# One more projection by seven half-size products: q of the second attention pattern

## The chip, the core and the metric

The kernel runs on one core of a Trainium2 chip. The core has a matrix engine (PE, whose weight loads are shown apart as PEld), three engines for elementwise work (DVE, ACT, POOL) and a queue engine (SP) that mainly issues DMAs; POOL issues DMAs as well. The engines run their instructions in order and wait for one another on semaphores. The metric is device time in microseconds. The kernel before took 2716.3 us, the median of three runs (2712.53, 2716.3 and 2717.81).

## The reference, cut to what matters

The program is a two-layer trunk on a sequence of 1024 rows of width 1024, all in float32. Layer 0 mixes tokens by a gated MLP, layer 1 by dilated attention; a squared-ReLU MLP follows each. The change lies in layer 1, in the making of q, k and v:

```
B_HEADS = 16                       # 64 wide each, so 8 pairs of heads
B_PATTERNS = ((128, 1), (512, 4), (2048, 16))     # window, dilation

def mixer_b(h, w_qkv, w_out, slopes):
    qkv = (h @ w_qkv).reshape(B, S, N_PAT, 3, B_HEADS, B_HEAD_DIM)
    for g, (window, dilation) in enumerate(B_PATTERNS):
        o, lse = dilated_branch(qkv[:, :, g, 0], qkv[:, :, g, 1], qkv[:, :, g, 2],
                                window, dilation, slopes)
```

There are three patterns g = 0, 1, 2, and for each a q, a k and a v: nine products of a 1024x1024 activation and a 1024x1024 piece of `w_qkv`. Pattern 1 has dilation 4: position s of the sequence stands in row i of residue r, with s = 4 i + r, and attention works on the residues apart. So its q, k and v are used in the order (r, i), here called the pattern's order.

## The kernel before, in words

Float32 products are made of three passes: each operand is split into a rounded part hi and a rest lo (`split`, line 100: ACT casts hi, then DVE subtracts to get lo), and hi*hi + hi*lo + lo*hi is summed in PSUM. A pass is a matmul of 128x128 by 128x512.

**The stage of v** (`values`, line 1157). v of all three patterns, and q and k of pattern 0, are made by a scheme of seven products of half-size blocks in place of eight (a Strassen scheme). `V_STEPS` (line 1145) lists (g, X, p): pattern g; X = 0, 1, 2 for q, k, v; p the product, in the order 1, 2, 5, 6, 7, 4, 3. One step is 4 blocks m of 12 matmuls, 48 in all, each block in its own PSUM bank. While step n runs, `right.prepare` makes the hi and lo of the next step's weights (two halves, at m = 0 and m = 2; tiles vrhi and vrlo), and `right.load` issues the loads of the step after. After products 1, 5 and 6 `evict` (line 1241) copies the bank to an SBUF tile (vpart); after 2, 7, 4 and 3 it adds that tile to the bank (not after 4, which is complete in its bank), splits the finished 128x512 block into hi and lo in a tile of the pool `parted` (line 1165, tag `vs`), and POOL stores the tile to DRAM. The pool `parted` has two buffers: the third finished block can be split only when the store of the first has landed. Finished blocks come in a burst of twelve, at the end of every group of seven products: four each after 7, 4 and 3.

**Attention** (`attention`, line 1300). It walks over 24 groups, for each pair of heads pattern 2, then 1, then 0 (`order`). A group has 8 slots of two halves. In a slot stand scores (PE), softmax (DVE and ACT), transposes (PE), their split (ACT, DVE) and the product with v (PE); `merge` joins the three patterns of a pair some slots later on DVE, by weights that go to DRAM and come back spread over partitions (`w_dram`, then the tiles bc). Between them `project` (line 1349) is a stream that makes q and k of patterns 1 and 2 pair by pair: one unit is q or k of one pattern and pair, 16 pieces of 3 matmuls (tiles psq and psk), with its weights loaded, split, and its result split in place into the tiles qhi, qlo, khi, klo in the pattern's order. There are 32 units, 512 pieces. 56 pieces (`lead`) run ahead of the first slot, and then the rest is dealt out evenly: in each half slot a credit of 512 - 56 = 456 is added and each piece costs 351, so 1.30 pieces stand in a half slot, until half slot 351. q and k of pattern 0 are loaded from DRAM, four blocks per pair (`load_block`).

The order on each engine is set by the program text and a scheduler that takes instructions by priority; the instructions marked `keep_in_program_order` stay where they are.

POOL's DMAs have a scratch that the kernel sets to 1024 bytes (`SCRATCH`, line 32, used in line 1843). In the attention pools qk[1] and qk[2], q and k of patterns 1 and 2 have one buffer for each tile.

Of the kernel before, what the change touches and what calls it, by code (L numbers as in the profile page):

```python
# [10 lines left out]
F32 = mybir.dt.float32  # L11
F32R = mybir.dt.float32r
# [23 lines left out]
def trunk(ctx: ExitStack, tc: tile.TileContext, x, c, ada_w, ada_b, ln_g, ln_b, a_w_in, a_b_in,  # L36
# [3 lines left out]
    nc = tc.nc  # L40
# [11 lines left out]
    dram = pool(ctx, "dram", 1, space=DRAM)  # L52
# [47 lines left out]
    def split(hi, lo, src, hi_engine=A, lo_engine=V):  # L100

        first = A.copy(hi, src) if hi_engine is A else hi_engine.tensor_copy(hi, src)  # L102
        return first, lo_engine.tensor_tensor(lo, src, hi, op=ALU.subtract)  # L103
# [994 lines left out]
    v_dram = [dram.tile([S, N_PAIRS, 4 * HEAD], F32, name=f"v_{g}") for g in range(3)]  # L1098

    qk_dram = dram.tile([N_PAIRS, 2, P, 2, S], F32, name="qk_0")  # L1100

    class RightForms:
        BLOCK = {1: (0, 0), 2: (1, 0), 5: (0, 1), 6: (1, 1), 7: (0, 1), 4: (1, 0)}
# [38 lines left out]
            split(hi[:], lo[:], r)  # L1142
            self.ready[g, X, p, kp] = hi, lo

    V_STEPS = [(g, X, p) for g, X in ((2, 2), (1, 2), (0, 2), (0, 0), (0, 1)) for p in (1, 2, 5, 6, 7, 4, 3)]

    def values_ahead(right):
        for kp in range(2):
            right.load(*V_STEPS[0], kp)
        yield  # L1150
        right.prepare(*V_STEPS[0], 0)
        right.load(*V_STEPS[1], 0)
        yield
        right.prepare(*V_STEPS[0], 1)
        right.load(*V_STEPS[1], 1)

    def values(before, right, ahead):
        run(ahead)
        form = before.form
        name = {1: "L11", 2: "L12", 5: "S1", 6: "S2", 7: "S3", 4: "L22", 3: "S4"}  # L1160
        with ExitStack() as ph:
# [3 lines left out]
            parted = pool(ph, "parted_v", 2)  # L1165
# [75 lines left out]
            def evict(g, X, p, m):  # L1241
                acc = sums["pb" if p in (2, 5, 3) else "pa", m][:]
                if p in (1, 5, 6):
                    t = parts[p, m] = x_tile(f"vpart_{g}_{X}_{p}_{m}")
                    A.copy(t[:], acc)
                    return
                if p != 4:
                    t = parts.pop(({2: 1, 7: 5, 3: 6}[p], m))
                    V.tensor_tensor(t[:], acc, t[:], op=ALU.add)  # L1249
                    acc = t[:]  # L1250
                half, dh = {2: (1, 0), 3: (1, 1), 4: (0, 0), 7: (0, 1)}[p]
                if X < 2:
                    t = parted.tile([P, 2, HALF], F32R, name=f"qs_{X}_{p}_{m}", tag="vs")
                    split(t[:, 0], t[:, 1], acc)
                    nc.gpsimd.dma_start(qk_dram[4 * dh + m, X, :, :, half * HALF : (half + 1) * HALF], t[:].bitcast(F32))
                    return
                v = parted.tile([P, 4, 4, HEAD], F32R, name=f"vs_{g}_{p}_{m}", tag="vs")
                split(v[:, :, 0:4:3, :], v[:, :, 1:3, :], acc.rearrange("p (h e c) -> p h e c", e=2, c=HEAD))
                i = 4 * half + m
                nc.gpsimd.dma_start(v_dram[g][i * P : (i + 1) * P, 4 * dh : 4 * dh + 4, :],  # L1260
                                  v[:].rearrange("p h f c -> p h (f c)").bitcast(F32))
# [36 lines left out]
    def attention(form):  # L1298
# [5 lines left out]
        with ExitStack() as ph:  # L1304
# [3 lines left out]
            qk = {g: pool(ph, f"attn_qk{g}", 1, side="right") for g in (1, 2)}  # L1308
# [33 lines left out]
            order = [(hp, g) for hp in range(N_PAIRS) for g in (2, 1, 0)]  # L1342
# [5 lines left out]

            def project():

                todo = [(n, X) for n in range(len(order)) if order[n][1] for X in range(2)]

                raw, units = {}, {}

# [17 lines left out]
                for i, (n, X), half in [(i, key, half) for i, key in enumerate(todo) for half in (1, 0)]:  # L1372
                    hp, g = order[n]
# [7 lines left out]
                    p = bank("mm", f"ps{nm}_{hp}_{g}_{half}")  # L1381
                    for k in range(KD):
# [3 lines left out]
                        if k == KD - 1:  # L1386
                            hi, lo = (perm(got[n][f"{nm}{m}"][:], g, half) for m in ("hi", "lo"))
# [21 lines left out]
            def attend(n, oT_of):  # L1409
                hp, g = order[n]  # L1410
                base = 8 * n
                my = got[n]
# [19 lines left out]
                last_one = n == len(order) - 1  # L1432
                groups = {0: ((0, 1), (2, 3), (4, 5), (6, 7)), 1: ((0, 1, 2), (3, 5), (4, 7, 6)), 2: ((0, 1, 2, 3), (4, 5, 6, 7))}[g]
                starts = {0: (0, 2, 3, 5) if last_one else (0, 2, 4, 6), 1: (0, 2, 5), 2: (0, 4)}[g]

                def load_block(m):
                    my[m] = []
# [355 lines left out]
            out_begin = begin()  # L1793

            stream = project()
            lead, credit = 7 * KD, 0
            for n in range(lead):
                next(stream)
                if 16 <= n < 20:
                    affine_load(n - 16)  # L1800
            due = 0
            for n, slot in enumerate(slots):
                for half, pos in enumerate(slot):
                    for _, f in sorted(pos, key=lambda x_: x_[0]):
                        f()
                    credit += 512 - lead
                    while credit >= 351:
                        credit -= 351
                        next(stream, None)
                    if n >= last_group - 8:  # L1810
                        due += 6
                        while due >= 8:
                            due -= 8
                            next(out_begin, None)
# [41 lines left out]
```

## Time and profile before

| | |
|---|---|
| three runs | 2712.53, 2716.3, 2717.81 us; median 2716.3 |
| profiled execution | 2717.79 us, its span 2716.1 us, mean granted clock of PE 0.996 |
| PE busy | 2655.5 us, 98% of the span |
| DVE, ACT, POOL busy | 1993.0, 1378.4, 114.9 us |
| stage of v | about 992 to 1379 us of the span |
| attention with its lead | from about 1379 us on |

In the profile L1283 stands for the matmuls of the stage of v (psv), L1384 for those of `project`, L102 and L103 for the two halves of every split, L1249 for the addition in `evict`, L1255 and L1260 for POOL's stores of q, k (tile qs) and v (tile vs). Busy time of PE counts pipelined matmuls from their start to a modelled end, so a PE that is 98% busy is one that seldom waits, and what a matmul costs is read from the distance between two starts, not from its duration.

### The profile page before, as it was taken

The page shows a single profiled execution, that of the slowest core. Times are in us where ns is not written, and L with a number is a line of the kernel's source. Part 1 is how long each engine was busy: PE and PEld are TensorE (multiplying, and loading weights), DVE is VectorE, ACT ScalarE, POOL GpSimd, SP SyncE. Part 2 cuts the span into 40 slices and gives each one's busy share as a digit, 9 for nine tenths or more (in the row PEclk, how much of TensorE's full clock was granted, in tenths as well). Part 3 has the DMA queues.
Part 4 walks back from the last instruction along what each step waited for, and adds up shares of the span by engine and source line. Part 5 has one row for each costly group of instructions (what it writes and reads, how often), then busy time and mean ns, then how long its engine had stood idle before and what let it go on. Part 6 is the DMA issues. An engine that isn't in the chain of part 4 may idle for free.

```text
span 2716.1 us, 37099 instructions
## 1 busy us (share of the span) xinstructions
PE 2655.5 (98%) x13242; PEld 2193.5 (81%) x13242; DVE 1993.0 (73%) x3610; ACT 1378.4 (51%) x2601; POOL 114.9 (4%) x193
## 2 busy tenths in 40 slices
PE   6999999999999999999999999999999999999998
PEld 5788887888788878888888888888887888878887
DVE  6787697777889778655647767777658966577877
ACT  3354375555444454433436666666645655544332
POOL 1000000000000001111111000000010000000000
PEclk9999999999999999999999999999999999999999
DMA  7534336667967745655475545554782654495562
GB/s 264 159 118 135 116 137 217 223 223 243 344 229 247 245 148 180 215 179 198 165 225 172 138 133 140 138 146 133 235 219 98 213 190 155 147 317 183 172 208 86
DMA packets 340781, 504.77 MB, mean 186 GB/s; under 512 B 51900, under 2 KB 177252, under 8 KB 340596
## 3 DMA queue, kind: packets, MB, share of 16 engines
q1 hardware_dynamic: 324212, 443.68, 51.5%
q0 software_dynamic: 16384, 58.73, 6.0%
q8 instruction: 104, 1.70, 0.3%
q14 instruction: 81, 0.66, 0.1%
HBM read 365.40 MB, written 136.92 MB: 185 GB/s over the span
## 4 chain that ended last, share of the span: by engine, by line
PE 76%; DVE 12%; DMA 6%; ACT 3%; issue 2%; SPq 0%; DVEq 0%; ACTq 0%
PE psd L957 22%; PE psv L1283 13%; PE psk L1384 6%; PE psq L1384 6%; PE psua L798 6%; DMA adaw<-in_ada_w_dram 3%; PE psd_wout L389 3%; PE pv L1553 3%; PE psuc L798 3%; PE psu L368 3%; PE sc L1473 3%; PE psv L470 2%; DVE adaacc L128 2%; DVE left L103 1%; PE pT L1526 1%
## 5 line engine op out<-in xcount | busy, mean ns | idle before, releaser
L798 PE MATMUL psua<-right,left 128*128 128x512 f32 x1536 | 364.8, 391 | 0.1
L957 PE MATMUL psd<-rhi,lhi 128*128 128x512 f32 x896 | 349.7, 390 | 3.0 <-ACT part L829 3.0
L957 PE MATMUL psd<-rlo,lhi 128*128 128x512 f32 x896 | 349.6, 390 | 0.2
L957 PE MATMUL psd<-rhi,llo 128*128 128x512 f32 x896 | 349.3, 390 | 0.0
L798 PEld LDWEIGHTS psua<-right,left 128*128 128x128 f32 x1536 | 288.3, 188 | 61.6 <-DVE right L103 1.2
L1495 ACT ACTIVATE p<-p,stat 128x128 f32<-128x128 f32 (+1 forms) x384 | 168.8, 441 | 96.8 <-DVE stat L1493 95.8
L957 PEld LDWEIGHTS psd<-rhi,lhi 128*128 128x128 f32 x896 | 168.6, 188 | 39.2 <-ACT part L829 3.9
L957 PEld LDWEIGHTS psd<-rlo,lhi 128*128 128x128 f32 x896 | 168.5, 188 | 35.9 <-DVE rlo L103 1.1
L957 PEld LDWEIGHTS psd<-rhi,llo 128*128 128x128 f32 x896 | 168.6, 188 | 34.9
L798 PE MATMUL psuc<-right,left 128*128 128x512 f32 x768 | 187.2, 390 | 0.0
L128 DVE SCALAR_TENSOR_TENSOR adaacc<-adaw,silu_c,adaacc 128x512 f32<-128x512 f32 x168 | 128.6, 775 | 59.6 <-DMA adaw<-in_ada_w_dram 59.0
L798 PEld LDWEIGHTS psuc<-right,left 128*128 128x128 f32 x768 | 143.6, 188 | 29.9 <-DVE right L103 0.2
L103 DVE TENSOR_TENSOR pTlo<-pT,pThi 128x512 fp32r<-128x512 f32 (+1 forms) x160 | 99.3, 621 | 75.9 <-ACT pThi L102 75.0
L103 DVE TENSOR_TENSOR left<-ws,left 128x512 fp32r<-128x512 f32 x128 | 87.9, 688 | 73.2 <-ACT left L102 71.3
L103 DVE TENSOR_TENSOR llo<-lraw,lhi 128x1024 fp32r<-128x1024 f32 x112 | 136.4, 1218 | 1.5 <-ACT lhi L102 1.5
L102 ACT CAST left<-ws 128x512 fp32r<-128x512 f32 x128 | 79.1, 620 | 104.5 <-DVE ws L719 92.0
L1384 PE MATMUL psk<-form_L,wqk_hi 128*128 128x512 f32 x384 | 126.9, 411 | 0.0
L1384 PE MATMUL psq<-form_L,wqk_hi 128*128 128x512 f32 x384 | 126.4, 410 | 0.0
L102 ACT CAST lhi<-lraw 128x1024 fp32r<-128x1024 f32 x112 | 117.3, 1047 | 9.3 <-PE psd L957 3.3
L1283 PE MATMUL psv<-vrhi,form_S 128*128 128x512 f32 x384 | 120.0, 391 | 1.3 <-DVE vpart L1249 0.8
L1493 DVE CUSTOM_DVE_ANT_0 p<-sc,bias 128x128 f32<-128x128 f32 (+1 forms) x384 | 113.7, 346 | 5.2 <-PE sc L1473 4.9
L102 ACT CAST pThi<-pT 128x512 fp32r<-128x512 f32 (+1 forms) x160 | 84.6, 530 | 60.4 <-PE pT L1526 43.3
(332 smaller groups left out, 6072.3 us busy)
## 6 DMA issues: line engine op xcount, KB each, us to landing
lraw<-forms SPq DMA_DIRECT2D x112, 512.0 KB
adaw<-in_ada_w_dram SPq DMA_DIRECT2D x192, 256.0 KB
up<-in_mlp_w_up_dram SPq DMA_DIRECT2D x64, 512.0 KB
forms<-s SPq DMA_DIRECT2D x128, 256.0 KB
rraw<-in_mlp_w_down_dram SPq DMA_DIRECT2D x64, 512.0 KB
forms<-part SPq DMA_DIRECT2D x96, 256.0 KB
v<-vs POOLq DMA_DIRECT2D x48, 512.0 KB, 3.7
vraw<-in_b_w_qkv_dram SPq DMA_DIRECT2D x42, 512.0 KB
```

Of the source, the lines that this page charges most:

```text
L102: first = A.copy(hi, src) if hi_engine is A else hi_engine.tensor_copy(hi, src)
L103: return first, lo_engine.tensor_tensor(lo, src, hi, op=ALU.subtract)
L128: ins = V.scalar_tensor_tensor(acc[:], raw[:], silu_c[:, k : k + 1], acc[:], ALU.mult, ALU.add)
L368: T.matmul(dst, s[a], m[b], start=(n == 0), stop=(n == last))
L389: T.matmul(p[:], stat[a][:, k, o : o + P], u[b][:, w], start=n == 0, stop=n == count - 1)
L798: T.matmul(acc, w[:, a, k, :], right[p][:, b, k, :], start=p in (1, 2, 5) and k + a + b == 0, stop=k == 3 and a == 1, skip_group_check=True)
L957: ins = T.matmul(sums[kind, m][:], l[a][:, k, m * P : (m + 1) * P], r[b][:, k, :], start=p in (1, 5, 2, 3) and kp + k + a + b == 0, stop=k ...
L1283: T.matmul(acc, rows[:, m * P : (m + 1) * P], cols_, start=p in (1, 2, 5) and kp + k + a + b == 0, stop=kp == 1 and k == 1 and a == 1, ski ...
L1384: T.matmul(p[:], wu[a][:, k * P : (k + 1) * P], h_op(k, half, b), start=k + c_ == 0, stop=k == KD - 1 and c_ == 2)
L1473: T.matmul(banks[e][:, sl], q_[a][rows, tq], k_[b][rows, keys], start=c_ == 0, stop=c_ == 2)
L1493: V.tensor_tensor_reduce(out=pr, in0=banks[e][:, sl], in1=st["bias"][:, width - w :], scale=-0.125, scalar=3e38, op0=ALU.add, op1=ALU.min, ...
L1495: A.activation(pr, pr, AF.Exp, bias=nm, scale=-1.0, accum_out=l)
```

## The change

q of pattern 1 leaves `project` and becomes a group of seven steps in `V_STEPS`, behind v of pattern 0 and ahead of q of pattern 0. A finished block is split with a strided reading of its source, so that hi and lo come out in the pattern's order, and is stored to a new DRAM tensor `q_1`, of [pair, 128, hi or lo, 1024]. The store's rows are four pieces of 128 numbers for each partition; it is issued as two DMAs, one for hi and one for lo. In attention `load_q` loads hi and lo of a pair, eight slots ahead of its group, into the same tiles qhi and qlo. `project` has 24 units (384 pieces) left; the lead is 40 pieces, and the credit deals out 328 pieces over the first 326 half slots and the last 16 over the next 25.

```
-    V_STEPS = [(g, X, p) for g, X in ((2, 2), (1, 2), (0, 2), (0, 0), (0, 1)) for p in (1, 2, 5, 6, 7, 4, 3)]
+    V_STEPS = [(g, X, p) for g, X in ((2, 2), (1, 2), (0, 2), (1, 0), (0, 0), (0, 1)) for p in (1, 2, 5, 6, 7, 4, 3)]
...
                 if X < 2:
-                    t = parted.tile([P, 2, HALF], F32R, name=f"qs_{X}_{p}_{m}", tag="vs")
+                    t = parted.tile([P, 2, HALF], F32R, name=f"qs_{g}_{X}_{p}_{m}", tag="vs")
+                    if g:
+                        hi, lo = (t[:, n].rearrange("p (r i) -> p r i", r=4) for n in range(2))
+                        split(hi, lo, acc.rearrange("p (i r) -> p r i", r=4))
+                        dst = q1_dram[4 * dh + m].rearrange("p a (r i) -> p a r i", r=4)
+                        for n in range(2):
+                            nc.gpsimd.dma_start(dst[:, n, :, half * P : (half + 1) * P], (hi, lo)[n].bitcast(F32))
+                        return
...
-                todo = [(n, X) for n in range(len(order)) if order[n][1] for X in range(2)]
+                todo = [(n, X) for n in range(len(order)) for X in {0: (), 1: (1,), 2: (0, 1)}[order[n][1]]]
...
+                @at(max(0, base - 8), 0)
+                def load_q():
+                    if g != 1:
+                        return
+                    for i, m in enumerate(("qhi", "qlo")):
+                        my[m] = qk[1].tile([P, S], F32R, name=f"{m}_{hp}_1", tag=m)
+                        nc.sync.dma_start(my[m][:].bitcast(F32), q1_dram[hp, :, i, :])
...
-            lead, credit = 7 * KD, 0
+            lead, credit = 5 * KD, 0
...
-                    credit += 512 - lead
-                    while credit >= 351:
-                        credit -= 351
+                    credit += (368 - lead) * 25 if 2 * n + half_of < 326 else 16 * 326
+                    while credit >= 326 * 25:
+                        credit -= 326 * 25
                         next(stream, None)
```

Three places show how the instructions stand. On POOL, at the end of v of pattern 0, before:

```order
L1260 DMA v_0_108<-vs_0_3_1_10256 128x1024
L1260 DMA v_0_108<-vs_0_3_2_10277 128x1024
L1260 DMA v_0_108<-vs_0_3_3_10296 128x1024
L1255 DMA qk_0_111<-qs_0_2_0_10391 256x1x512
L1255 DMA qk_0_111<-qs_0_2_1_10410 256x1x512
```

The same place now, where "128x4x128 x2" are the two DMAs of one block, hi and lo:

```order
L1268 DMA v_0_108<-vs_0_3_2_10278 128x1024
L1268 DMA v_0_108<-vs_0_3_3_10297 128x1024
L1260 DMA q_1_112<-qs_1_0_2_0_10392 128x4x128 x2
L1260 DMA q_1_112<-qs_1_0_2_1_10412 128x4x128 x2
L1260 DMA q_1_112<-qs_1_0_2_2_10436 128x4x128 x2
L1260 DMA q_1_112<-qs_1_0_2_3_10456 128x4x128 x2
L1260 DMA q_1_112<-qs_1_0_7_0_10623 128x4x128 x2
```

Sixteen blocks of q, each with two DMAs of 512 pieces of 512 bytes, have come in ahead of the stores of pattern 0, whose blocks are one DMA of 256 pieces.

On ACT, in the new group: the burst of finished blocks (qs) after products 7, 4 and 3, and between them the casts of the weights of later steps (vrhi_1_0_3: product 3 of the new group; vrhi_0_0_1 and vrhi_0_0_2: products 1 and 2 of q of pattern 0, the next group).

```order
L102 CAST qs_1_0_7_0_10623<-vpart_1_0_5_0_10479 128x512
L102 CAST qs_1_0_7_1_10641<-vpart_1_0_5_1_10496 128x512
L102 CAST qs_1_0_7_2_10664<-vpart_1_0_5_2_10516 128x512
L102 CAST vrhi_1_0_3_0_10687<-v_r22_0_8564 128x1024
L102 CAST vrhi_1_0_3_1_10726<-v_r22_1_8565 128x1024
L102 CAST qs_1_0_7_3_10682<-vpart_1_0_5_3_10533 128x512
L102 CAST qs_1_0_4_0_10703<-psv1_1_0_0_10305 128x512
L102 CAST qs_1_0_4_1_10721<-psv1_1_0_1_10322 128x512
L102 CAST qs_1_0_4_2_10742<-psv1_1_0_2_10341 128x512
L102 CAST vrhi_0_0_1_0_10765<-v_t_0_8562 128x1024
L102 CAST vrhi_0_0_1_1_10807<-v_t_1_8563 128x1024
L102 CAST qs_1_0_4_3_10760<-psv1_1_0_3_10358 128x512
```

The pattern goes on with the first three blocks of product 3 (qs_1_0_3_0 to qs_1_0_3_2), then vrhi_0_0_2_0 and vrhi_0_0_2_1, then the last block. So the weights of product 2 of the next group stand on ACT behind the eleventh block of the burst. For v of pattern 0 the order before is the same, with vs in place of qs.

On PE, in attention, in the fourth pair of heads (psk: pieces of `project`; pT: transposes; pv: product with v), before:

```order
L1384 MATMUL psk_4_2_1_14836<-form_L12_8185,wqk_17_hi_14625 128x512 x2
L1384 MATMUL psk_4_2_1_14836<-form_L12_8185,wqk_17_lo_14626 128x512
L1553 MATMUL pv_6_1_0_14947<-pThi_6_1_0_14887,v_3_1_14666 128x256
L1553 MATMUL pv_6_1_0_14947<-pTlo_6_1_0_14888,v_3_1_14666 128x256
L1553 MATMUL pv_6_1_0_14947<-pThi_6_1_0_14887,v_3_1_14666 128x128
L1553 MATMUL pv_6_1_0_14947<-pTlo_6_1_0_14888,v_3_1_14666 128x128
L1384 MATMUL psk_4_2_0_14953<-form_S1_8627,wqk_17_hi_14625 128x512 x2
L1384 MATMUL psk_4_2_0_14953<-form_S1_8627,wqk_17_lo_14626 128x512
L1384 MATMUL psk_4_2_0_14953<-form_S1_8627,wqk_17_hi_14625 128x512 x2
L1384 MATMUL psk_4_2_0_14953<-form_S1_8627,wqk_17_lo_14626 128x512
L1526 MATMUL pT_6_1_2_14960<-ident_73,p_6_1_4_14891 128x128
L1529 MATMUL pT_6_1_2_14960<-ident_73,p_6_1_5_14803 128x128
```

And now:

```order
L1392 MATMUL psk_4_2_1_15153<-form_L12_8186,wqk_13_hi_14919 128x512 x2
L1392 MATMUL psk_4_2_1_15153<-form_L12_8186,wqk_13_lo_14920 128x512
L1569 MATMUL pv_6_1_0_15256<-pThi_6_1_0_15201,v_3_1_14986 128x256
L1569 MATMUL pv_6_1_0_15256<-pTlo_6_1_0_15202,v_3_1_14986 128x256
L1569 MATMUL pv_6_1_0_15256<-pThi_6_1_0_15201,v_3_1_14986 128x128
L1569 MATMUL pv_6_1_0_15256<-pTlo_6_1_0_15202,v_3_1_14986 128x128
L1392 MATMUL psk_4_2_1_15153<-form_L12_8186,wqk_13_hi_14919 128x512 x2
L1392 MATMUL psk_4_2_1_15153<-form_L12_8186,wqk_13_lo_14920 128x512
L1542 MATMUL pT_6_1_2_15265<-ident_73,p_6_1_4_15205 128x128
L1545 MATMUL pT_6_1_2_15265<-ident_73,p_6_1_5_15120 128x128
```

One piece of `project` stands in each half slot where there were one or two; the rest of the row is unchanged.

More of the change, by code (lines that the diff above doesn't have):

```diff
@@ L1100, in trunk @@
     qk_dram = dram.tile([N_PAIRS, 2, P, 2, S], F32, name="qk_0")
+    q1_dram = dram.tile([N_PAIRS, P, 2, S], F32, name="q_1")
     class RightForms:
@@ L1802, in attention @@
             for n, slot in enumerate(slots):
-                for half, pos in enumerate(slot):
+                for half_of, pos in enumerate(slot):
                     for _, f in sorted(pos, key=lambda x_: x_[0]):
                         f()
-                    credit += 512 - lead
-                    while credit >= 351:
-                        credit -= 351
+                    credit += (368 - lead) * 25 if 2 * n + half_of < 326 else 16 * 326
+                    while credit >= 326 * 25:
+                        credit -= 326 * 25
                         next(stream, None)
```

## The prediction

> **What bounds the kernel now.** I read first the table of busy time by stretch, then the chain that ended last, then POOL's timeline and the landing times of its stores.
>
> The table has for each stretch its length and then the busy time of PE, PEld, DVE, ACT and POOL, the granted clock and the DMA share: two stretches of the stage of v, four pairs of attention, and one twelfth of a pair.
>
> ```profile
> 985.00:1250.00 265.00, 263.67 (x1176) 217.05 (x1175) 185.36 (x244) 122.69 (x175) 26.98 (x50) 1.00 0.57 197
> 1250.00:1385.00 135.00, 135.00 (x597) 111.79 (x596) 71.35 (x87) 55.58 (x78) 21.51 (x32) 1.00 0.56 194
> 1500.00:1900.00 400.00, 399.54 (x2707) 336.58 (x2706) 287.40 (x897) 257.16 (x770) 11.79 (x32) 1.00 0.52 140
> 1598.20:1604.40 6.20, 6.20 (x47) 5.18 (x46) 6.04 (x14) 3.47 (x12) 0.00 (x0) 1.00 0.34 92
> ```
>
> In both stages PE is busy to the last per cent at full clock: whatever takes PE work away shortens the kernel, unless another engine makes PE wait. In attention DVE is at 72% and ACT at 64%, but once in a pair DVE is full (6.04 of 6.20 us). The chain gives PE's true price, in consecutive matmuls of one kind:
>
> ```profile
> 1044.59 334.92 PE psv L1283 x1476
> 1379.51 10.88 PE psq L1384 x48
> ...
> 1561.05 1.49 PE sc L1473 x24
> ...
> 1572.45 1.44 PE psk L1384 x6
> ...
> 1613.80 1.40 PE psq L1384 x6
> ...
> 1859.27 1.49 PE sc L1473 x24
> ```
>
> A matmul costs 334.92 / 1476 = 0.227 us in the stage of v and 10.88 / 48 = 0.227 in the lead; in bursts of six between small matmuls 1.40 to 1.44, so 0.233 to 0.240. The first scores of the second and sixth pair stand 298.2 us apart, so a pair takes 74.6 us.
>
> **PE's sum.** Removed: eight units of 48 matmuls, 384. At 0.227 they cost 87.1 us, at 0.240 92.2. Added: seven steps of 48, 336 x 0.227 = 76.3 us; a step takes 10.9. The difference is 11 to 16 us; the bursts don't vanish but get shorter, which keeps part of their switching, so I take **-13 us**.
>
> **The stores of the new blocks.** This is what I expect to decide. The rows of POOL's DMAs before (count, busy, mean ns; KB and median us to landing; the third line, of the stores of q and k, min/median/max), of the ACT casts that wait for them, and of the work of one finished block:
>
> ```profile
> L1260 POOL DMA_DIRECT2D v<-vs x48 | 25.6, 533 | 277.1 <-DVE vs L103 277.1
> L1255 POOL DMA_DIRECT2D qk<-qs x32 | 21.8, 682 | 131.5 <-DVE qs L103 130.6 <-DVE far L1319 0.9
> DMA to landing us min/median/max: 3.0/3.8/8.9
> v<-vs POOLq DMA_DIRECT2D x48, 512.0 KB, 3.7
> wo_parts<-wo_hi POOLq DMA_DIRECT2D x16, 256.0 KB, 5.0
> ACT vs L102 <- DMA v<-vs: 44.0, 21, 5.7
> L1249 DVE TENSOR_TENSOR vpart<-psv,vpart 128x512 f32<-128x512 f32 x60 | 41.1, 685 | 6.3 <-PE psv L1283 6.3
> L102 ACT CAST vs<-vpart 128x512 fp32r<-128x512 f32 x36 | 22.4, 621 | 56.2 <-DVE vpart L1249 27.9 <-DMA v<-vs 18.8 <-DVE vraw L1136 3.7
> L103 DVE TENSOR_TENSOR vs<-vpart,vs 128x512 fp32r<-128x512 f32 x36 | 24.8, 689 | 10.8 <-ACT vs L102 10.8
> L102 ACT CAST vrhi<-v_t 128x1024 fp32r<-128x1024 f32 x28 | 29.2, 1053 | 8.1 <-PE psv L1283 8.1
> L103 DVE TENSOR_TENSOR vrlo<-v_t,vrhi 128x1024 fp32r<-128x1024 f32 x28 | 34.2, 1221 | 18.0 <-ACT vrhi L102 18.0
> ```
>
> And a burst of twelve on POOL's timeline (start, duration), v of pattern 0, with the two closest stores of the next group:
>
> ```profile
> 1199.82 0.53 POOL L1260 DMA_DIRECT2D v<-vs  x1 [22.17 <-DVE vs L103]
> ...
> 1233.01 0.54 POOL L1260 DMA_DIRECT2D v<-vs  x1 [2.93 <-DVE vs L103]
> ...
> 1293.12 0.68 POOL L1255 DMA_DIRECT2D qk<-qs  x1 [5.62 <-DVE qs L103]
> 1294.36 0.68 POOL L1255 DMA_DIRECT2D qk<-qs  x1 [0.56 <-DVE qs L103]
> ```
>
> PE finishes a block in 12 x 0.227 = 2.72 us. Twelve stores in 33.2 us are one in 3.02: two buffers and one store of 3.7 us for each block are already a little slower than PE, and ACT waits for landings 21 times, 44 us in all. PE doesn't feel it, because the weights that ACT makes are ahead. Now each block has two DMAs, of four times the pieces in all (1024 of 512 bytes for 256 of 2 KB).
>
> Call c the time in which the stores of one block go through. The buffer of block k comes free when block k-2 has landed, so if the first store of the burst starts at 0, block 11 is cast at 9c. Behind block 11 on ACT stand the weights of product 2 of the next group. PE wants these 38 us after the first store: product 7's step begins about 5 us before that store (12 matmuls 2.7, addition 0.69, cast 0.62, subtraction 0.69, and the hand-overs), and products 7, 4, 3 and the next 1 are four steps, 43.5. After block 11's cast come two more casts (2.1) and the subtractions (1.22 each, behind the block's own), about 4 us until PE's first block of that step can run through. So PE loses **9c + 4 - 38 = 9c - 34 us**, and nothing as long as c is under 3.8.
>
> What c is, no row shows; it depends on whether POOL gets a second such store under way while the first is out. Low end: it does. POOL's issue goes from 533 ns for 128 pieces to 682 for 256, so some 0.98 for 512; a buffer's round is 0.62 + 0.69 + 2 x 0.98 + 3.7 = 7.0 us for two blocks' worth of buffers, c = 3.5, no loss. High end: each of the two is alone and takes as long as the 256 KB stores to wo_parts, 5.0: c = 10, a loss of 56 us. Between them, one at a time at the smallest landing, 3.0: c = 6.0, a loss of 20; at 3.7: c = 7.4, a loss of 33. I take one at a time, by the nearest rows: the most that is ever in flight before is two stores of 256 pieces (1293.12 and 1294.36, each out for at least 3.0 us), 512 pieces, and one new store alone has 512, in a scratch that the kernel keeps at 1024 bytes. And I take 3.7 for one: half the bytes, but 0.3 us more issue. **+33 us**, with 0 and 56 as ends.
>
> The Trainium skill has a figure for such a DMA ("DMA: Bandwidth & Descriptors", Anatomy of one DMA — SWDGE (gpsimd) path): about 2.0 us and the bytes at 436 GB/s, with the cost of descriptors small. For the 512 KB stores that is an estimate of 3.2 us where the row has 3.8, issue included; for 256 KB it would be 2.6, c = 5.2, a loss of 13 and a sum of 2722 us. The same page (Terms; The descriptor swizzle) has a descriptor of 16 bytes, a transfer's descriptors spread over 16 engines and one more on each for its completion, and "SBUF — State Buffer" (SBUF size) calls the scratch the carveout of these descriptor rings. An estimate from these: 512 / 16 + 1 = 33 descriptors for one new store, 66 for two, where 1024 bytes hold 64, and 17 for a store of 256 pieces. By that rule the second store waits; no run so far shows it.
>
> The other costs of the new steps lie under PE: DVE's eight subtractions and fourteen vrlo at 1.22, twelve additions and sixteen splits at 0.69, some 46 us of 76, like the steps beside them (71.35 of 135). Reading with a stride of 16 bytes costs more, as merge's products show (the larger two are the strided patterns): 1.07 for 0.67 us, twelve times 0.4 at most, also covered. Twelve more weight loads of 512 KB go through SP in 76 us, the rate of the other groups, whose matmuls don't wait for them.
>
> ```profile
> L1649 DVE TENSOR_TENSOR bc<-oT,bc x48: 669/1067/1105, 1522.0 to 2038.6; 128x512 f32<-128x512 f32 x48
> ...
> DVE bc L1649 <- DMA bc<-w_dram: 3.4, 1, 3.4
> L103 DVE TENSOR_TENSOR qlo<-psq,qhi 128x512 fp32r<-128x512 f32 x32 | 22.1, 689 | 15.2 <-ACT qhi L102 14.9
> L103 DVE TENSOR_TENSOR wqk_lo<-wq_raw,wqk_hi 128x1024 fp32r<-128x1024 f32 x16 | 19.6, 1225 | 12.7 <-ACT wqk_hi L102 12.4
> ```
>
> **Attention with less PE work.** A pair loses 48 x 0.24 = 11.5 us of PE, 74.6 to 63.1. DVE has 0.72 x 74.6 = 53.6 us of work there and loses a weight split and two result splits, 1.22 + 2 x 0.69 = 2.6: 51.0 of 63.1, 81%. ACT comes to about 72%. So PE still binds over a pair, but the twelfth in which DVE was full (6.04 us) now has 5.25 us of PE: DVE falls back by 0.8 us there, and the weights of merge, which DVE waited for once before (3.4 us), come relatively later, as their DMA round doesn't shrink. Price: 0 if the banks between absorb it, up to 2.5 us in seven pairs if not, 17; I take **+4**. The 16 loads of q are 512 KB each, in place of 8 weight loads; they are issued eight slots, some 21 us, ahead of use, and what they wait for (scores of the pair before, stores of the stage of v) is long past: 0, at most one exposed landing at the first pair, 4.
>
> **Sum.** 2717.8 us (the profiled execution: span 2716.1 and 1.7 around it) - 13 + 33 + 4 = 2741.8. That execution lies 1.5 above the median shown, so 2740 against 2716.3: **slower by 0.9%**.
>
> **Rivals.** *The stores overlap* (faster): POOL keeps both in flight, c is 3.5, and only -13 + 4 is left: about 2707. For it: two stores of 256 pieces do overlap. Against: never more than 512 pieces. It decides at c = 3.8 for the stall, and at c = 4.8 the gain is just eaten (9 x 4.8 - 34 = 9). *One at a time, but short* (3.0 or less each, the bytes being half): c = 6, 2716.3 - 13 + 20 + 4 = 2727. The Trainium skill's figure named above ("DMA: Bandwidth & Descriptors", the same section) belongs to this case. *DVE becomes the bound of attention*, with one at a time: the full twelfth and merge's round cost 17 in place of 4: 2753. *The change doesn't do what it says*, because attention isn't bound by PE: 399.54 of 400 us speaks against it; it gets no chance of its own.
>
> **How the numbers follow.** A measurement of this kernel can tell 0.2%, 5.4 us, from no change. One at a time near 3.7: 0.5 (2732 to 2750). One at a time and short: 0.2 (2722 to 2732). DVE-bound besides: 0.1 (2750 to 2760). Stores overlapping: 0.15 (2702 to 2711). Something between, within 5.4 us: 0.05. Slower is then 0.5 + 0.2 + 0.1 less 0.01 for the short end: 0.79; faster 0.15; same 0.06. The range reaches from within the overlapping case to within the DVE-bound one, 2706 to 2757; the likeliest sign's own range is 2722 to 2757.
>
> **What would show it.** In the stage of v: POOL's stores of q_1 in pairs, the second 3 to 4 us behind the first, sixteen blocks some 7.4 us apart in the burst; ACT's cast of qs waiting for them some 50 us in all; PE idle or stretched by about 33 us, most of it ahead of products 1 and 2 of q of pattern 0. Wrong, if POOL's two DMAs start about 1 us apart and PE runs through; then the total is below 2716. In attention: a pair near 63 to 65 us with PE busy near 100%. Over 66, DVE has taken over.

## The result, and the profile after

The changed kernel takes 2750.7 us (median; 2748.5 to 2759.7), the kernel before 2717.0 in the runs beside it: **1.0136 times as long, 95% interval 1.0124 to 1.0148**, so 34 us slower. The profiled execution took 2752.4 us, 34.6 more than the one of before. Slower was forecast, and the time lies in the range, but 11 us above the forecast of 2740; two terms of the sum had the wrong size, in opposite directions.

First the table of busy time by stretch, for the stage of v and for attention (first projection to last scores), of the kernel before. The stage of v is counted here from two groups of transposes that stand 18 us ahead of its first matmul. The columns are as in the prediction: length, busy time of PE, PEld, DVE, ACT and POOL, granted clock, DMA share.

```profile
974.10:1379.35 405.25, 402.44 (x1790) 332.00 (x1789) 263.10 (x344) 180.12 (x256) 47.59 (x80) 1.00 0.55 192
1379.35:2001.59 622.24, 620.83 (x4101) 521.39 (x4099) 430.13 (x1293) 383.60 (x1133) 32.78 (x64) 1.00 0.58 162
```

The same two stretches of the changed kernel, and then four pairs of attention and one piece of a pair:

```profile
970.89:1475.94 505.05, 486.37 (x2124) 398.82 (x2125) 311.43 (x394) 214.90 (x298) 71.78 (x112) 0.98 0.52 182
1475.94:2038.76 562.82, 544.05 (x3717) 452.82 (x3715) 408.00 (x1269) 366.72 (x1109) 32.81 (x64) 0.99 0.65 187
1641.86:1910.66 268.80, 261.43 (x1840) 218.54 (x1839) 203.80 (x649) 184.56 (x561) 8.82 (x24) 1.00 0.59 164
1653.58:1661.61 8.03, 7.57 (x52) 6.17 (x50) 7.14 (x33) 5.32 (x21) 0.81 (x2) 1.00 0.49 135
```

Length minus PE's busy time is PE's idle time. The stage of v is 99.8 us longer: 83.9 more of busy PE and 15.9 more of idle PE (18.68 for 2.81). Attention is 59.4 us shorter: 76.8 less busy, but 17.4 more idle (18.77 for 1.41). That makes +40.4. The rest, -5.9, lies ahead of the stage of v (it starts 3.2 us earlier) and behind attention (2.7 us shorter), where the programs are alike.

A pair takes 268.80 / 4 = 67.2 us, where 63.1 was forecast and 74.6 was before. DVE's share in a pair is 76%, but in the last row, 8 us long, it is 7.14 of 8.03.

In the stage of v POOL's timeline (start, duration, idle before and its releaser) has the stores of q_1 one by one; behind it stand the summary of this group of stores and the waits between 1285 and 1360 us (total, times, longest):

```profile
1296.04 0.76 POOL L1260 DMA_DIRECT2D q<-qs  x1 [2.70 <-issue]
1298.89 0.77 POOL L1260 DMA_DIRECT2D q<-qs  x1 [2.09 <-issue]
1301.74 0.76 POOL L1260 DMA_DIRECT2D q<-qs  x1 [2.09 <-issue]
1304.63 0.75 POOL L1260 DMA_DIRECT2D q<-qs  x1 [2.13 <-issue]
```

```profile
L1260 POOL DMA_DIRECT2D q<-qs x32: 750/755/782, 1240.3 to 1345.4; - x32
...
  ACT qs L102: 58.9, 13
...
DMA to landing us min/median/max: 2.5/2.6/5.4
```

```profile
ACT qs L102 <- DMA q<-qs: 47.9, 10, 5.8
...
PE psv L1291 <- ACT vrhi L102: 12.4, 2, 6.5
...
PE psv L1291 <- DVE vrlo L103: 3.0, 1, 3.0
```

One store starts every 2.85 us, 0.3 after the median landing of the one before; the idle time between has, in these rows, no releaser in the program ("issue"). ACT waits for landings, and the weights behind its casts come late: PE waits 5.9, 3.0 and 6.5 us. PE's timeline around the first two of these waits shows something that the forecast did not have:

```profile
1299.25 0.62 PE L1291 MATMUL psv<-form_S,vrhi 128*128 128x512 f32 x2
...
1306.01 1.22 PE L1291 MATMUL psv<-form_L,vrhi 128*128 128x512 f32 x2 [5.92 <-ACT vrhi L102]
...
1307.86 1.05 PE L1291 MATMUL psv<-form_L,vrhi 128*128 128x512 f32 x2
...
1312.93 0.79 PE L1291 MATMUL psv<-form_L,vrlo 128*128 128x512 f32 x1 [3.03 <-DVE vrlo L103]
1313.52 1.05 PE L1291 MATMUL psv<-form_L,vrhi 128*128 128x512 f32 x2
```

Two matmuls take 0.62 us ahead of the wait and 1.05 behind it. In the windows 1313.00 to 1316.00 and 1338.00 to 1342.00 (behind the second wait, and 8 us behind the end of the third) PE's clock is 0.50 and 1.00:

```profile
1313.00:1316.00 3.00, 3.00 (x7) 2.41 (x8) 1.61 (x2) 0.00 (x0) 0.76 (x1) 0.50 0.30 98
...
1338.00:1342.00 4.00, 4.00 (x19) 3.33 (x18) 2.64 (x3) 3.62 (x6) 0.76 (x1) 1.00 0.32 131
```

In attention the groups of PE over the same four pairs (busy, mean ns, then idle before and what ended it) show where PE waits: 2.8, 0.5 and 4.1 us. Ahead of them stand the same groups in the kernel before, over its four pairs from 1561.00 to 1859.20 us, and PE's busy time there:

```profile
1561.00:1859.20 298.20, 297.74 (x2011) 250.55 (x2010) 214.83 (x661) 192.03 (x571) 8.81 (x24) 1.00 0.52 142
L1553 PE MATMUL pv<-pTlo,v 128*128 128x128 f32 (+1 forms) x200 | 47.1, 278 | 0.4 <-DVE pTlo L103 0.3
L1553 PE MATMUL pv<-pThi,v 128*128 128x128 f32 (+1 forms) x200 | 45.8, 261 | 0.0
...
L1529 PE MATMUL pT<-ident,p 128*128 128x128 f32 x88 | 22.8, 273 | 0.1
```

```profile
L1569 PE MATMUL pv<-pTlo,v 128*128 128x128 f32 (+1 forms) x200 | 47.5, 280 | 2.8 <-DVE pTlo L103 2.7
L1569 PE MATMUL pv<-pThi,v 128*128 128x128 f32 (+1 forms) x200 | 46.6, 264 | 0.5 <-ACT pThi L102 0.4
...
L1545 PE MATMUL pT<-ident,p 128*128 128x128 f32 x88 | 23.1, 275 | 4.1 <-ACT p L1511 4.1
```

### The profile page after: what moved, and what is told of

It is laid out like the page before. It is cut to its first block, busy times and chain, and to the rows that moved or that the text cites. A ratio compares the mean times of both kernels' runs of the same rounds, so it can differ in the third digit from the quotient of the medians.

```text
span 2750.6 us, 37193 instructions
## 1 busy us (share of the span) xinstructions
PE 2659.4 (97%) x13194; PEld 2189.8 (80%) x13194; DVE 2019.4 (73%) x3636; ACT 1396.0 (51%) x2619; POOL 139.1 (5%) x225
## 4 chain that ended last, share of the span: by engine, by line
PE 46%; issue 26%; DVE 14%; ACT 5%; DMA 5%; POOL 3%; SPq 0%; POOLq 0%; DVEq 0%; ACTq 0%
PE psd L957 13%; PE psua L798 7%; PE psuc L798 3%; PE psu L368 3%; PE psk L1392 3%; PE psd_wout L389 3%; DMA adaw<-in_ada_w_dram 3%; PE psq L1392 2%; PE pv L1569 2%; ACT p L1511 2%; PE sc L1489 1%; PE psub L798 1%; DVE adaacc L128 1%; DVE left L103 1%; DVE pTlo L103 1%
## 5 line engine op out<-in xcount | busy, mean ns | idle before, releaser
L1291 PE MATMUL psv<-form_S,vrhi 128*128 128x512 f32 x384 | 118.5, 390 | 0.4 <-DVE vpart L1250 0.4
L102 ACT CAST rhi<-rraw 128x1024 fp32r<-128x1024 f32 x48 | 50.5, 1052 | 115.1 <-issue 76.8
```

Source lines behind the costliest of these rows:

```text
L1291: T.matmul(acc, rows[:, m * P : (m + 1) * P], cols_, start=p in (1, 2, 5) and kp + k + a + b == 0, stop=kp == 1 and k == 1 and a == 1, ski ...
```

## The experiments

**The two halves apart, and the stores.** Four kernels on one chip; the kernel before took 2718.8 us there.

`scratch1280` gives POOL's DMAs more room:

```diff
-SCRATCH = 1024
+SCRATCH = 1280
```

> The changed kernel with 1280 bytes of POOL's DMA scratch in place of 1024, nothing else. Theory (the scratch lets only one 512-piece store out at a time): with 1280 two fit (66 descriptors, by the estimate of the prediction, of 80), the two stores of a block start about 1 us apart, PE's three waits of 5.9, 3.0 and 6.5 us ahead of q of pattern 0 and the half clock behind them go, the stage of v is 23 us shorter, total about 2728 (2724 to 2732). Rival (one store of 512-byte pieces at a time is what the memory or the DMA engines take, whatever room the queue has): the second store may start earlier but lands no earlier, total 2748 to 2753 as the changed kernel.

Measured: 2731.9 us, 1.0036 times before (1.0025 to 1.0047). The second store of a block now mostly starts 0.8 to 1.1 us after the first, as expected (two rows show pairs back to back), and ACT's waits for them fall from 58.9 to 19.0 us (its timeline, the group's waiters, and its two stretches):

```profile
1295.74 1.51 POOL L1260 DMA_DIRECT2D q<-qs  x2 [4.05 <-issue]
...
1304.62 1.53 POOL L1260 DMA_DIRECT2D q<-qs  x2 [2.40 <-issue]
```

```profile
  ACT qs L102: 19.0, 6
```

```profile
979.18:1461.64 482.46, 479.38 (x2126) 395.07 (x2126) 311.94 (x394) 215.21 (x298) 71.67 (x112) 1.00 0.55 191
1461.64:2022.03 560.39, 541.22 (x3717) 450.49 (x3715) 407.91 (x1269) 366.71 (x1109) 32.80 (x64) 1.00 0.66 187
```

The stage of v is 22.6 us shorter, its idle time 3.1 us, its clock 1.00. So room in POOL's scratch limited the stores: 256 bytes more take the whole stall away. The whole kernel gains 19 us by the medians and 27 by the two ratios, around what the stage shows.

`lo_on_sp` stores the low halves through another queue:

```diff
-                            nc.gpsimd.dma_start(dst[:, n, :, half * P : (half + 1) * P], (hi, lo)[n].bitcast(F32))
+                            (nc.gpsimd, nc.sync)[n].dma_start(dst[:, n, :, half * P : (half + 1) * P], (hi, lo)[n].bitcast(F32))
```

> The changed kernel with the low half of each q_1 block stored through SP's queue, the high half through POOL's. Theory (POOL's queue is the limit): each block costs POOL one store, 2.9 us from start to start, under the 3.8 at which the stall begins, so the 23 us go, total about 2728. Against it SP now waits in its queue for each split, and the weight loads behind it start later; if they become late, PE waits for weights and part of the 23 us stays (2730 to 2745). Rival (the memory takes one such store at a time): nothing gained, 2748 or more.

Measured: 2731.1 us, 1.0040 (1.0023 to 1.0057). The stall goes here too, and the weight loads behind the stores on SP do not become late:

```profile
971.21:1452.43 481.22, 478.48 (x2125) 395.23 (x2125) 311.68 (x394) 215.64 (x298) 59.16 (x96) 1.00 0.56 191
1452.43:2011.97 559.54, 541.20 (x3717) 450.38 (x3715) 408.07 (x1270) 366.48 (x1109) 33.28 (x65) 1.00 0.66 188
```

PE's busy time without the stall, 478.48 - 402.44 = 76.0 us, is what the seven steps cost in matmuls (forecast 76.3). The changed kernel's 486.37 hold 7.9 more: most of it is half clock behind the waits, where 29 steps from one matmul to the next took 6.9 us more than at 0.227.

`v_only` is the kernel before with the new steps and their stores, which nobody reads:

```diff
-    V_STEPS = [(g, X, p) for g, X in ((2, 2), (1, 2), (0, 2), (0, 0), (0, 1)) for p in (1, 2, 5, 6, 7, 4, 3)]
+    V_STEPS = [(g, X, p) for g, X in ((2, 2), (1, 2), (0, 2), (1, 0), (0, 0), (0, 1)) for p in (1, 2, 5, 6, 7, 4, 3)]
...
```

> The kernel before with the seven steps of q of pattern 1 and their stores beside v; attention is as before and makes its own q of pattern 1, so the new q_1 is stored and not read. Theory (the two halves add up): the stage of v grows as in the changed kernel by 99.8 us, less the 3 us by which it began earlier there, and attention stays at 74.6 us a pair: 2717 + 97 to 100 = 2814 to 2817. Rival (part of the growth of attention's cost comes from the stores or the start): attention changes as well, and the total leaves 2810 to 2820.

`attn_only` is the changed kernel without them:

```diff
-    V_STEPS = [(g, X, p) for g, X in ((2, 2), (1, 2), (0, 2), (1, 0), (0, 0), (0, 1)) for p in (1, 2, 5, 6, 7, 4, 3)]
+    V_STEPS = [(g, X, p) for g, X in ((2, 2), (1, 2), (0, 2), (0, 0), (0, 1)) for p in (1, 2, 5, 6, 7, 4, 3)]
...
-                        nc.sync.dma_start(my[m][:].bitcast(F32), q1_dram[hp, :, i, :])
+                        nc.sync.dma_start(my[m][:].bitcast(F32), qk_dram[hp, 0, :, i, :])
```

> The changed kernel without the seven steps beside v and their stores: attention loads q of pattern 0 in the place of q of pattern 1 (same bytes and shape, so scores of pattern 1 are of other numbers). Theory (a pair keeps 67 us because its own chain of DVE, ACT and PE is late, whatever lies ahead): 67 us a pair, the waits of about 1.0 us ahead of the transposes and 0.4 to 0.5 ahead of the weighted sums stay, total 2751 - 99 = 2652 (2648 to 2656). Rival (the waits come from the loads of q_1 or from the late start of attention): a pair near 64.5, total about 2633.

Measured: `v_only` 2820.1 us, 1.0365 (1.0348 to 1.0382), so +101 in its own comparison, just above the expected 2814 to 2817; PE idles 3.7 us in its attention. `attn_only` 2657.5 us, 0.9758 (0.9741 to 0.9776), -61, just above the expected range's end of 2656. Its pairs take the same time as in the changed kernel, and PE idles almost as long in attention. The stretches of attention in the two:

```profile
1479.44:2104.01 624.57, 620.86 (x4101) 521.34 (x4099) 430.05 (x1293) 384.09 (x1133) 32.76 (x64) 1.00 0.58 162
```

```profile
1374.88:1932.53 557.65, 540.85 (x3717) 450.58 (x3715) 408.61 (x1269) 366.73 (x1109) 32.78 (x64) 1.00 0.67 188
```

The two halves add up within their intervals (+101 - 61 = +40; the stages of the two traces gave +40.4, the medians +34). And attention's waits come neither from the stores nor from a late start: they are attention's own (16.8 us idle with no new store in the program).

**What PE waits for in attention.** Theory 1 was distance (three half-slots between transposes and weighted sums, each now shorter), theory 2 DVE: stretches in which it is full. The kernel before took 2714.3 us on this chip.

`then4`:

```diff
-                            then = half_slot + 3
+                            then = half_slot + 4
```

> The changed kernel with the weighted sums four half-slots behind their transposes in place of three (in all pairs but the last pattern). In the changed kernel PE is idle 18.8 us in attention, mostly 0.4 to 0.5 us ahead of the weighted sums (pThi, pTlo late) and 1.0 us ahead of one transpose a pair (p late). Theory 1 (a half-slot has become 1.40 us where it was 1.55, and three of them no longer hold the way transposes, cast, subtraction): the waits ahead of the weighted sums go, some 0.9 us a pair and some small ones that show as longer matmuls, about 10 us in all, total 2740; the 1.0 ahead of the transposes stays. Theory 2 (DVE is full for 8 us at a stretch where those waits are, so the data are late by whatever is queued ahead of them): the waits move or shrink a little, total 2746 to 2751.

Measured: 2755.1 us, 1.0146 (1.0128 to 1.0164), no better than the changed kernel's 1.0136. The waits at the weighted sums shrink, and the one at the transposes takes their place (groups of PE over four pairs):

```profile
L1569 PE MATMUL pv<-pTlo,v 128*128 128x128 f32 (+1 forms) x200 | 48.0, 283 | 1.2 <-DVE pTlo L103 1.0
...
L1545 PE MATMUL pT<-ident,p 128*128 128x128 f32 x88 | 23.6, 280 | 7.4 <-ACT p L1511 7.4
```

Theory 1, which expected 2740, falls: more distance gains nothing.

`spread` moves, on top of `lo_on_sp`, merge's factors with their reading, the products and sums on the residual's rows, and the last scores of pattern 0:

```diff
-                starts = {0: (0, 2, 3, 5) if last_one else (0, 2, 4, 6), 1: (0, 2, 5), 2: (0, 4)}[g]
+                starts = {0: (0, 2, 3, 5) if last_one else (0, 2, 4, 5), 1: (0, 2, 5), 2: (0, 4)}[g]
...
-                @at(*((base + 4, 0) if hp < N_PAIRS - 1 else (base + 1, 1)))
+                @at(*((base + 6, 0) if hp < N_PAIRS - 1 else (base + 1, 1)))
                 def factors():
...
-                @at(*((base + 4, 1) if hp < N_PAIRS - 1 else (base + 1, 1)))
+                @at(*((base + 6, 1) if hp < N_PAIRS - 1 else (base + 1, 1)))
                 def spread():
...
-                    at(5 * i - 15, 0)(lambda i=i: affine_load(i))
-                at(*((i + 1, 1) if i < 4 else (5 * i - 12, 1)))(lambda i=i: affine_row(i))
+                    at(5 * i - 11, 0)(lambda i=i: affine_load(i))
+                at(*((3 * i + 1 + (i > 1), 1) if i < 4 else (5 * i - 8, 1)))(lambda i=i: affine_row(i))
```

> The changed kernel with the low halves stored through SP, as in lo_on_sp, and three groups of DVE's work in attention moved: the factors of merge and their reading two slots later, away from the softmax of pattern 2; the eight products and sums on the residual's rows of the first slots spread over twelve slots; the last scores of pattern 0 one slot earlier. Theory 2 (the waits come from stretches in which DVE is full): the first pair's waits (2.0, 0.5, 0.8 us) and the half clock behind them, some 5 us, go; the 0.5 ahead of pattern 2's weighted sums and the 1.0 ahead of pattern 0's transposes go in each pair: idle time of PE in attention from 18.3 to 6 or less, total 15 to 19 us under lo_on_sp's 2731, 2712 to 2716, so about what the kernel before takes. Theory 1 (the distance in half-slots is too short): idle stays over 12 us, total 2724 or more.

`spread_then4` has both edits:

> The kernel of spread with the weighted sums four half-slots behind as in then4. If both theories hold a part, PE's idle time in attention falls to 3 us or less and the total to 2708 to 2712, under the kernel before; if theory 2 is all, as spread, 2712 to 2716; if the longer distance makes gathers late, above spread.

Measured: `spread` 2729.7 us, 1.0059 (1.0044 to 1.0074); `spread_then4` 2731.8, 1.0067 (1.0052 to 1.0082). Theory 2 as I had put it missed (2712 to 2716). The numbers given for theory 1 came in `spread`, but `then4` had already spoken against its mechanism, and `spread_then4`, with the longer distance, is no faster. Idle time of PE in attention stays at 18.9 us in `spread` and rises to 24.7 in the other. The wait at the transposes is gone and a new one stands at the scores of pattern 0, which need the banks that DVE's softmax has not yet read (`spread`, four pairs):

```profile
L1569 PE MATMUL pv<-pTlo,v 128*128 128x128 f32 (+1 forms) x200 | 47.7, 281 | 2.8 <-DVE pTlo L103 2.7
L1569 PE MATMUL pv<-pThi,v 128*128 128x128 f32 (+1 forms) x200 | 46.7, 264 | 1.8 <-ACT pThi L102 1.7
...
L1489 PE MATMUL sc<-bk,bq 64*128 64x256 f32 (+1 forms) x192 | 16.9, 294 | 4.2 <-DVE stat L1509 4.2
```

Moving one piece of DVE's work or one of its readers only moves the wait. That left two questions: is it DVE's load at all, and can PE's work be moved instead? The next three were on a chip on which the kernel before took 2712.6 us.

`no_sums` takes load from DVE and nothing else:

```diff
-                steps = [lambda f=f, g=g, half=half: f(g, half) for f, g in pieces for half in range(2)]
+                steps = [lambda f=f, g=g, half=half: f(g, half) if f is cut or g == 0 else None for f, g in pieces for half in range(2)]
```

> The changed kernel with part of merge left out: for seven pairs the products of patterns 2 and 1 with their factors, and the two sums, so the merged rows hold pattern 0 alone. DVE has 4 x 1.07 + 4 x 0.69 = 7.0 us less in each of these pairs, 51.0 to 44.0 of 67 us; PE's, ACT's and the DMAs' work is the same. Theory 2 (DVE's load sets the pair once PE has less): PE's idle time in attention falls from 18.8 to 8 us or less, a pair from 67 to 65, total 2735 to 2741. Rival (the way from scores through softmax to transposes and back to the next scores is a chain of latencies, with only two banks for scores; DVE's load elsewhere doesn't matter): idle stays over 15 us, total 2747 or more.

Measured: 2736.1 us, 1.0084 (1.0068 to 1.0101), about 14 us under the changed kernel. Attention is 15.5 us shorter, and PE idles 10.0 us in it in place of 18.8, a little over the 8 expected; all of attention, and four pairs:

```profile
1476.97:2024.31 547.34, 537.29 (x3717) 450.18 (x3715) 366.54 (x1213) 365.79 (x1109) 33.10 (x65) 1.00 0.67 192
1638.69:1899.55 260.86, 258.69 (x1840) 218.53 (x1839) 180.93 (x617) 184.79 (x561) 8.81 (x24) 1.00 0.61 170
```

A pair takes 65.2 us, and PE's busy time falls too, from 261.43 to 258.69, though its work is the same; I take that for small waits that had been counted as busy. With DVE at 69% of a pair in place of 76%, PE's idle time in the four pairs falls from 7.4 to 2.2 us, and in all of attention by nearly half. So most of what PE waits for inside the pairs is DVE's load.

`paced`, on top of `lo_on_sp`, leaves DVE's work as it is and puts PE's work where DVE is full:

```diff
+            MOVED = {4: -1, 6: -1, 13: 1, 14: 1, 17: -1, 18: -1, 20: -1, 27: 1, 44: 1, 45: 1}
...
+                    if 2 * n + half_of < 288:
+                        credit += 326 * 25 * MOVED.get((2 * n + half_of) % 48, 0)
```

> The kernel lo_on_sp with ten of the 48 pieces of projection (three matmuls, 0.7 us each) of each of the first six pairs in other half-slots: five taken from half-slots 4, 6, 17, 18 and 20, in which DVE is least busy, and put into 13, 14, 27, 44 and 45, just ahead of PE's waits. Theory (PE's waits sit where DVE is full for some us; PE work put there fills them, and DVE catches up): idle in attention from 18.3 to 10 us or less, total 2721 to 2725. Rival (a wait taken away at one place comes back at the next, as in spread): idle over 15, total 2728 to 2733 as lo_on_sp.

`paced_rows` adds the rows of `spread`:

> The kernel paced with the products and sums on the residual's rows spread over the first slots as in spread. Theory: the first pair's waits of 2.0 and 0.5 us go, and the half clock behind them; 4 to 6 us under paced, so 2716 to 2721 if paced does what its theory says. Rival: they come back two to three slots later, no difference to paced within 3 us.

Measured: `paced` 2714.8 us, 1.0006 (0.9995 to 1.0018): **as fast as the kernel before**. `paced_rows` 2719.3, 1.0029 (1.0019 to 1.0039), so spreading the rows hurts. In `paced` attention and four pairs are:

```profile
1451.23:2000.89 549.66, 538.70 (x3717) 449.23 (x3715) 408.26 (x1269) 365.78 (x1109) 33.84 (x65) 1.00 0.67 191
1609.05:1873.90 264.85, 261.34 (x1840) 218.56 (x1839) 204.16 (x649) 184.15 (x561) 9.65 (x24) 1.00 0.60 167
```

Idle time in attention is 11.0 us for 18.3 in `lo_on_sp`, on the same work of every engine. The gain over `lo_on_sp` is 9.9 us in attention and as much in the medians, each against its own kernel before (+2.2 for +12.2). In `paced_rows` three rows' products and sums now stand among the softmaxes of pattern 1 in the first pair: DVE is busy without a break from 1501 to 1513 us, PE waits 1.9 and 1.1 us behind it, and its clock is 0.56 and 0.50 in the next ten (1517.00 to 1527.00):

```profile
1517.00:1522.00 5.00, 3.91 (x16) 2.99 (x18) 2.58 (x5) 1.38 (x3) 0.00 (x0) 0.56 0.62 207
1522.00:1527.00 5.00, 5.00 (x24) 4.09 (x22) 1.69 (x9) 2.15 (x9) 0.00 (x0) 0.50 0.81 218
```

**Larger bursts.** Two last kernels, with the kernel before at 2716.0 us.

`bursts`, on top of `lo_on_sp`:

```diff
-                    while credit >= 326 * 25:
+                    while credit >= 326 * 25 and (half_of == 0 or 2 * n + half_of >= 326):
```

> The kernel lo_on_sp with the pieces of projection issued two at a time, six matmuls in every first half of a slot and none in the second, in place of three in each half. In the changed kernel projection stands in 40 places of PE's program a pair, and a matmul of it costs 0.249 us by PE's steps where it is 0.227 in long runs: some 3 us of switching a pair. Theory (the switching is paid by the place): with a third fewer places 0.5 to 1 us a pair is saved, and four pieces in place of three lie between transposes and weighted sums, so the 0.4 to 0.5 us waits there go: 1.5 to 2 us a pair, total 2716 to 2721 against 2731 of lo_on_sp. Rival (DVE's full stretches come first; larger bursts make the data of the small matmuls later): 2728 or more.

`bursts_paced` moves two pieces a pair besides (`MOVED = {4: -1, 18: -1, 28: 1, 44: 1}`):

> The kernel bursts with two of its 48 pieces a pair moved in the first six pairs, from half-slots 4 and 18 to 28 and 44, as in paced. Theory: both gains add, total 2708 to 2713, so at or just under the kernel before (2712 to 2717 in the runs so far). Rival (paced and bursts fill the same waits): no better than paced, 2714 to 2720.

Measured: `bursts` 2728.1 us, 1.0048 (1.0031 to 1.0065): the rival, the transposes now wait 6.0 us over four pairs. `bursts_paced` 2718.2, 1.0009 (1.0000 to 1.0019): no better than `paced`. Halving the places at which projection stands in PE's program saved 0.4 us of its 36.1 us a pair (sum of PE's steps from one matmul's end to the next), and 0.8 in `bursts_paced`. Of these 36.1 us some 3.2 are above the price of 0.227 a matmul, and with 21 places a pair in place of 40 still 2.8: most of that surcharge isn't paid by the place, and what it is paid for stays open. No version here beats the kernel before.

## Why the prediction was right, and where its sum was off

- **That the stores decide the stage of v: right.** One store at a time, ACT's casts waiting, PE idle ahead of products 1 and 2 of q of pattern 0: all as forecast, and both ways of giving the stores more room removed it. ACT waited 58.9 us for "some 50".
- **The size of that term, +33: too high, and for the wrong reason in part.** A landing takes 2.6 us, not 3.7; with the hand-over a store costs 2.85 us and c is 5.7 in place of 7.4. The formula 9c - 34 then gives 17 us, and PE idled 15.9 longer. What it lacked is the clock: behind each of these waits PE ran at 0.50, and the stage has 7.9 us more of busy PE. Together 23.8. The split is the trace's; 9c - 34 is the whole delay at product 2, with the slow matmuls ahead of it inside, so a match within 2 us doesn't prove the formula. PE's first two waits (5.9 and 3.0 us) stand at product 1 and the third (6.5) ahead of product 2. The Trainium skill's figure ("DMA: Bandwidth & Descriptors", Anatomy of one DMA — SWDGE (gpsimd) path) gave an estimate of 2.6 us for a store, which the trace agrees with; I had set it aside for a row of stores of twice the bytes. The estimate of 66 descriptors against 64, from the same page of the Trainium skill (Terms; The descriptor swizzle), agrees with the runs as well: 1024 bytes hold one such store, 1280 (80) hold two. Two sizes only bracket the limit; they don't show that it counts descriptors.
- **Attention with less PE work, +4: this step failed.** The prediction had "PE still binds over a pair" and a price of "0 if the banks between absorb it", up to 17 if not. The full stretch was seen (6.04 of 6.20 us of DVE), but priced as one slip of 0.8 us a pair. It cost 17.4 us of idle PE and, by `paced`'s busy time (538.70 for 544.05), 5.4 of half clock and hidden small waits: 22.7, and nearer 29 by the next point. DVE is at 76% of the shorter pair, and what counts are stretches such as the 8 us shown, at nine tenths, with a reader of DVE's or ACT's work on PE behind them. This is the rival "DVE becomes the bound of attention", which was given 0.1 with a price of 17, and its mark, a pair over 66 us, is what came. `no_sums` shows the cause by taking load from DVE, `paced` by filling the full stretches.
- **The work, -13: about right, though PE's busy time says half of it.** Added 76.0 (forecast 76.3). Busy PE in attention fell by 620.83 - 538.70 = 82.1 even in `paced`, where 87 to 92 was forecast, so -6.1. But PE's steps on projection fell from 45.9 us for 187.5 matmuls a pair to 36.1 for 144.75: 0.230 for each that is gone, 88.5 for 384, and -12.5. The rest is in the other matmuls, whose work is the same: in four pairs PE's busy time less these steps is 113.9 us before, 117.0 in the changed kernel and in `paced`, and 114.3 in `no_sums`. It mostly goes with DVE's load in `no_sums`, so I read it as waiting on DVE that is counted as busy, which belongs to the point above.
- **The sum.** By busy time -6.1 + 23.8 + 22.7, by PE's steps -12.5 + 23.8 + 29.1: both +40.4 in the two stages, with -5.9 outside them, so +34.6 between the two profiled executions. That the forecast of +24 came within 11 us is in part luck: the stores were some 9 us too high, attention 19 to 25 too low, and the -5.9 nobody had forecast. I take the part outside for variation between executions: the stage of v starts anywhere between 969.85 and 979.18 us in the kernels shown here, with the same program ahead of it.
- **The rivals.** Stores that overlap: false with 1024 bytes of scratch, true with 1280; but the 2707 us given for that case would not have come, since `scratch1280` still takes 2731.9. *One at a time, but short* was right on the stores, and too low in all for want of attention's waits and the clock.

## What to carry to other kernels

Work moved off the bound engine is worth its time only where the other engines have room in each stretch, not on average: look for stretches of several microseconds in which another engine is over 90% busy, and expect the bound engine to wait behind them. Such waits wander when one reader or one producer is moved; what helped here was to redistribute the bound engine's own filler work, five pieces of 48, which alone won some 10 us. And when one transfer becomes two with smaller pieces, count the pieces in flight against the queue's room, not the bytes.

## What the runs showed of the hardware

A wait of PE costs more than its length. Behind 5.9, 3.0 and 6.5 us the clock was 0.50 for 3.5, 3.2 and about 6 us (matmuls 0.427 us apart in place of 0.227). The Trainium skill has this ("TensorE: Matmul & The Clock Gate", Part 1: The HAM clock gate, What's actually happening): half clock after an idle window of about 3.4 us, full clock after about as much sustained work. The trace agrees with the length of the window: the half clock sets in during the wait and lasts 6.8, 3.4 and 10.2 us in all, multiples of 3.41. It doesn't agree that a wait must be so long. The one of 3.0 us was enough, and so were two of 2.0 and 0.5 us in the first pair of attention, with work between them. There the 3.41 us ahead of the drop held 1.42 us of busy PE, and the half clock (columns as above) lasted 10.24:

```profile
1520.75 0.33 PE L1569 MATMUL pv<-pThi,v 128*128 128x128 f32 x1 [1.99 <-ACT pThi L102]
1521.61 0.47 PE L1569 MATMUL pv<-pTlo,v 128*128 128x128 f32 x1 [0.53 <-DVE pTlo L103]
```

```profile
1517.63:1521.04 3.41, 1.42 (x6) 0.75 (x5) 3.38 (x13) 3.07 (x15) 2.52 (x2) 1.00 0.84 240
1521.04:1531.28 10.24, 9.71 (x42) 8.05 (x42) 5.96 (x18) 4.38 (x15) 0.74 (x2) 0.50 0.18 54
1531.28:1534.70 3.42, 3.42 (x30) 2.89 (x29) 1.59 (x3) 1.17 (x2) 0.54 (x1) 1.00 0.37 153
```

In `lo_on_sp` the same two waits, of 2.00 and 0.53 us at 1495.7 and 1498.0, cost one stretch of 3.41 us at half clock (1499.72 to 1503.13). So the price of a short wait can't be read from its length; what decides it is not shown.

POOL's issue of a store grew less with its pieces than I had estimated: 755 ns for 512 pieces, beside 533 for 128 and 682 for 256. And a store for which its queue has no room shows in the profile as POOL's idle time under "issue", with no releaser: that word can hide a full queue.
